# Seven-product up projections: one PSUM bank that sums four products, weights split 1024 wide, and context vectors left out of a modulation

## The chip, the cores and the metric

The kernel runs on one core of a Trainium2 chip. The core's engines work side by side, each through its own queue in order: TensorE (PE) multiplies matrices into PSUM, an accumulator memory of eight banks here; VectorE (DVE) and ScalarE (ACT) do elementwise work between PSUM and SBUF; SyncE (SP) issues the loads. The metric is device microseconds (us) of one execution, as the median of several runs.

## The reference

Two layers over 512 latent tokens and 256 context tokens of width 1024. Each layer has a gated feed-forward block (FFN), a mixer (attention in the first layer, gated linear attention in the second) and another FFN; each adds to the stream through a gate, after a norm with shift and scale that depend on conditioning vectors.

```python
def swiglu(h, w_gu, w_down):
    gu = h @ w_gu
    return (jax.nn.silu(gu[..., :D_FF]) * gu[..., D_FF:]) @ w_down

def pre_mod(t, m, norm_g, i):
    h = rms_norm(t, norm_g[i]) * (1.0 + m[..., 3 * i + 1, :]) + m[..., 3 * i, :]
    return h, m[..., 3 * i + 2, :]

    mod = (jax.nn.silu(c) @ p["w_mod"] + p["b_mod"])          # latent tokens
    mod_c = (jax.nn.silu(c_ctx) @ p["w_mod"] + p["b_mod"])    # context tokens
    h, gt = pre_mod(x, mod, ng, 0)
    x = x + 0.5 * gt * swiglu(h, p["ffn1_w_gu"], p["ffn1_w_down"])
    # ... mixer with ng[1]; FFN 2 with ng[2]; the same for context tokens with mod_c.
    # In the last layer context tokens get no mixer output and no second FFN.
```

`D_FF` is 2816, so a hidden dimension of 22 blocks of 128. Everything is computed in float32 accuracy.

## The kernel before

**Products.** Each float32 operand is split in a high part (rounded, by ScalarE, L127) and a low part (the rest, by VectorE, L128); a product is high x high, high x low and low x high. A weight therefore arrives by DMA in a `raw` tile, and `split` makes `whi` and `wlo` from it. The pool `stage` holds three buffers each of `raw`, `whi` and `wlo`, all [128, 1024], and serves up projections, down projections and projections of the mixers.

**The four FFN stages** (`ffn`) have their units at 117 to 522, 1074 to 1480, 1593 to 1998 and 2408 to 2673 us of the profiled execution. The first three work on all 768 tokens, the last on 512. Within a stage the 22 hidden blocks go in four parts of 6, 6, 5 and 5 (`PARTS`): first the up projections of a part's blocks, then the part's down projections (`pair`, L374), whose results `add_gated` (L398) adds to the stream. The last part's down projections are in `close_out`, which also prepares what follows. From the fifth hidden block on (the sixth in the last stage) the up projection of a block is a `unit`: the weight block A (gate and up columns, two `raw` tiles of 1024) and the activations B are cut in four quarters each, and seven products of quarter sums take the place of eight. The quarter sums of B are made once per stage (T1 to T4); those of A (S1 to S4) in each unit. A product is 4 x 3 matmuls (`product`, L602) of 384 columns, 256 in the last stage: 84 matmuls a unit.

**A unit before** takes four banks (`a` to `d`) of a ring of eight. Two products accumulate in each of `a`, `c` and `d`; one stands in `b`. VectorE makes S1 to S4 in small tiles (L624) and each quarter is split on its own, 512 columns at a time. ScalarE copies the first product of `a` and of `c` to `v` (L641, L643), VectorE adds the others (`add`, L639, and L648), silu is done in `sg` (L651, L654), one VectorE product of 768 columns joins both halves (L658), and `split` makes the hidden block's `dh` and `dl`, which the down projections read.

**The modulation** is worked out piecemeal beside all this: `mod_step` (L278) takes pieces from `pending` at a rate `bg` per unit or down projection, loads 256 KB (`wm`), and has VectorE reduce it against each of two vectors, latent and context (`junk`, L297).

**The order.** The code is written unit by unit, and a scheduler then orders each engine's instructions by its own estimate of times. So matmuls of a next unit may stand between those of the present one. Engines wait for each other where a tile is read, and where its buffer was used before.

Of the kernel before, what the change touches and what calls it, by code (L numbers as in the profile page):

```python
# [8 lines left out]
F32 = mybir.dt.float32  # L9
# [38 lines left out]
class Net:  # L48
# [123 lines left out]
    def mod_finish(self, l, p):  # L172
# [4 lines left out]
        for v in range(2):  # L177
# [4 lines left out]
        if p % 3 == 2 and p != 5:  # L182
            nc.vector.tensor_scalar(out=m, in0=m, scalar1=0.5, scalar2=None, op0=ALU.mult)

# [93 lines left out]
    def mod_step(self, n):  # L278
        nc = self.nc
        self.owed += n  # L280
        while self.owed >= 1 and self.pending:
            self.owed -= 1
            l, p, m, i = self.pending.pop(0)
            if i == 0 and m == 0 and p == 0:
                nc.sync.dma_start(out=self.bmod[l], in_=self.ins[f"b_mod{l}"])
                nc.sync.dma_start(out=self.ng[l], in_=self.ins[f"norm_g{l}"])
# [7 lines left out]
            for v in range(2):  # L294
# [4 lines left out]
            if i and m == KT - 1:  # L299
                nc.vector.tensor_tensor(out=self.mod[l][p], in0=self.mod[l][p], in1=self.acc, op=ALU.add)  # L300
# [151 lines left out]
    def ffn(self, l, sub, idx, segs, nxt, bg=(0, 0), first=4, start=False):  # L452
# [12 lines left out]
        st = ExitStack()  # L465
        with st:
# [52 lines left out]
            for pi, (f0, nf) in enumerate(PARTS):  # L519
                for f in range(f0, f0 + nf):  # L520
                    if f >= early:
                        if f >= first:
# [6 lines left out]
                            seven(sp, gu[f], sg, hid[f])  # L529
# [22 lines left out]
    def seven_open(self, st, h, n0):  # L552
# [7 lines left out]
        sub = lambda o, a, b: nc.vector.tensor_tensor(out=o, in0=a, in1=b, op=ALU.subtract)  # L560

# [26 lines left out]
        def weights(a):  # L588
            hi = self.stage.tile([128, 1024], F32R, tag="whi", name="whi", bufs=3)
            lo = self.stage.tile([128, 1024], F32R, tag="wlo", name="wlo", bufs=3)  # L590
            res = []
            for i, x in enumerate(a):
                c = slice(i * 512, (i + 1) * 512)
                self.split(x(), hi[:, c], lo[:, c])
                res.append((hi[:, c], lo[:, c]))
            return res
# [21 lines left out]
        def unit(sp, src, sg, hid):  # L618
            A11, A12, A21, A22 = [x[:, i:i + 512] for x in [self.raw(src[:, j:j + 1024]) for j in (0, 1024)] for i in (0, 512)]

            def comb(a, b, op):
                def f():
                    o = sp.tile([128, 512], F32, tag="s", name="s", bufs=2)
                    nc.vector.tensor_tensor(out=o, in0=a, in1=b, op=op)  # L624
                    f.out = o
                    return o
                return f
            s1 = comb(A21, A22, ALU.add)
            wA11, wS1 = weights([lambda: A11, s1])
            s2 = comb(s1.out, A11, ALU.subtract)  # L630
# [1200 lines left out]
```

## Time and profile before

| | |
|---|---|
| median of 3 runs | 2709.84 us (2709.37 to 2710.6) |
| profiled execution | 2708.46 us |
| its span, first to last instruction | 2706.7 us |
| mean granted TensorE clock | 0.990 |
| TensorE busy | 2617.1 us (97%) |
| VectorE busy | 2161.1 us (80%) |
| ScalarE busy | 1196.9 us (44%) |
| GpSimd busy | 171.6 us (6%) |
| data moved | 279.31 MB, mean 103 GB/s |

Times of single instructions come from the profiled execution; its time is 1.4 us under the median. Matmuls overlap one another, so their pace is read from one start to the next and not from a duration. "Idle before" in a row is the time for which the engine stood still ahead of that instruction, and the name behind the arrow is what released it. In the mixers TensorE has many small holes; in the FFN stages it has few.

### The profile page before, as it was taken

To read this page: it belongs to the slowest core of one execution; us is meant where nothing else is said; L and a number is where in the kernel's file an instruction comes from. 1 tells how busy PE (TensorE), PEld (TensorE's weight loads), DVE (VectorE), ACT (ScalarE), POOL (GpSimd) and SP (SyncE) were. 2 spreads that over 40 slices of the span, in tenths; PEclk is the share of its full clock that TensorE was granted. 3 is DMA by queue.
4 is the path that set the end of the run, shared out by engine and by line. 5 is a ranking of instruction groups with operands and counts; after the bars stand their busy time and mean duration, and the time that the engine had idled before them with its cause. 6 is when DMAs were issued, how large, how long until landed. Compare 5 with 4: busy or idle time off the path is not lost. (4 is left out here: it accounts for less than half of the span.)

```text
span 2706.7 us, 44030 instructions
## 1 busy us (share of the span) xinstructions
PE 2617.1 (97%) x16800; PEld 2435.1 (90%) x16800; DVE 2161.1 (80%) x4503; ACT 1196.9 (44%) x2254; POOL 171.6 (6%) x206
## 2 busy tenths in 40 slices
PE   7999999999878899999999999999999999999999
PEld 5899999989777789899999999999998998989899
DVE  6789798977888867797988878888777677778677
ACT  4324242445757744242424542424345565435344
POOL 0000000013443200000000000000000121000000
PEclk9999999999989999999999999999999999999999
DMA  8143444431000140433343314343232121422334
GB/s 313 42 150 115 139 132 145 124 126 42 24 24 1 47 141 30 129 114 127 117 141 100 115 63 138 108 145 104 92 116 86 56 71 63 148 71 92 102 106 128
DMA packets 103572, 279.31 MB, mean 103 GB/s; under 512 B 12256, under 2 KB 15200, under 8 KB 101824
## 3 DMA queue, kind: packets, MB, share of 16 engines
q1 hardware_dynamic: 103360, 276.50, 31.4%
q8 instruction: 132, 2.16, 0.3%
q14 instruction: 80, 0.66, 0.1%
HBM read 269.11 MB, written 7.34 MB: 102 GB/s over the span
## 5 line engine op out<-in xcount | busy, mean ns | idle before, releaser
L127 ACT ACTIVATE whi<-raw 128x512 fp32r<-128x512 f32 (+3 forms) x466 | 355.7, 767 | 739.9 <-PE r L374 326.4
L128 DVE TENSOR_TENSOR wlo<-raw,whi 128x512 fp32r<-128x512 f32 (+3 forms) x466 | 399.2, 859 | 81.0 <-ACT whi L127 78.2
L602 PE MATMUL r<-t,whi 128*128 128x384 f32 (+1 forms) x1704 | 400.9, 323 | 1.8 <-DVE u L639 1.3
L602 PE MATMUL r<-hh,wlo 128*128 128x384 f32 (+1 forms) x1136 | 366.1, 323 | 0.0
L602 PE MATMUL r<-hh,whi 128*128 128x384 f32 (+1 forms) x1136 | 365.8, 322 | 0.0
L602 PE MATMUL r<-hl,whi 128*128 128x384 f32 (+1 forms) x1136 | 365.7, 322 | 0.0
L297 DVE SCALAR_TENSOR_TENSOR junk<-wm,cb 128x512 bf16<-128x512 f32 x480 | 329.1, 686 | 13.4 <-ACT cb L276 8.3
L602 PEld LDWEIGHTS r<-t,whi 128*128 128x128 f32 x1704 | 295.6, 188 | 3.2 <-DVE u L639 2.1
L602 PE MATMUL r<-t,wlo 128*128 128x384 f32 (+1 forms) x852 | 273.3, 323 | 0.0
L374 PE MATMUL r<-dh,whi 128*128 128x512 f32 (+1 forms) x952 | 267.3, 345 | 0.8 <-ACT whi L127 0.8
L374 PE MATMUL r<-dh,wlo 128*128 128x512 f32 (+1 forms) x952 | 266.8, 346 | 0.3 <-DVE wlo L128 0.3
L374 PE MATMUL r<-dl,whi 128*128 128x512 f32 (+1 forms) x952 | 266.8, 344 | 0.0
L127 ACT ACTIVATE whi<-s 128x512 fp32r<-128x512 f32 x284 | 174.6, 625 | 182.4 <-DVE s L624 67.0
L602 PEld LDWEIGHTS r<-hl,whi 128*128 128x128 f32 x1136 | 213.4, 188 | 0.8
L602 PEld LDWEIGHTS r<-hh,wlo 128*128 128x128 f32 x1136 | 213.4, 188 | 0.4 <-DVE wlo L128 0.4
L602 PEld LDWEIGHTS r<-hh,whi 128*128 128x128 f32 x1136 | 213.3, 188 | 0.3
L374 PEld LDWEIGHTS r<-dh,wlo 128*128 128x128 f32 x952 | 178.6, 188 | 24.4 <-DVE wlo L128 1.1
L374 PEld LDWEIGHTS r<-dh,whi 128*128 128x128 f32 x952 | 178.0, 188 | 24.5 <-ACT whi L127 2.7
L374 PEld LDWEIGHTS r<-dl,whi 128*128 128x128 f32 x952 | 178.1, 188 | 23.5
L128 DVE TENSOR_TENSOR wlo<-s,whi 128x512 fp32r<-128x512 f32 x284 | 190.7, 684 | 4.4 <-ACT whi L127 3.7
L398 DVE SCALAR_TENSOR_TENSOR x<-r,mod,x 128x512 f32<-128x512 f32 (+1 forms) x168 | 100.1, 632 | 90.8 <-PE r L374 90.3
L602 PEld LDWEIGHTS r<-t,wlo 128*128 128x128 f32 x852 | 159.9, 188 | 0.1
(417 smaller groups left out, 5845.1 us busy)
## 6 DMA issues: line engine op xcount, KB each, us to landing
raw<-gu SPq DMA_DIRECT2D x176, 512.0 KB, 3.9
wm<-w_mod SPq DMA_DIRECT2D x240, 256.0 KB, 2.9
raw<-dn SPq DMA_DIRECT2D x88, 320.0 KB, 2.9
raw<-dn SPq DMA_DIRECT2D x64, 384.0 KB, 3.1
raw<-w_out SPq DMA_DIRECT2D x28, 512.0 KB, 3.8
m<-w_mod0a SPq DMA_DIRECT2D x12, 1024.0 KB, 10.4
raw<-w_in SPq DMA_DIRECT2D x8, 512.0 KB, 4.8
raw<-w_kq SPq DMA_DIRECT2D x8, 512.0 KB, 3.7
```

What stands on the lines that cost most here:

```text
L127: self.nc.scalar.activation(out=hi, in_=src, func=AF.Copy)
L128: (e or self.nc.vector).tensor_tensor(out=lo, in0=src, in1=hi.bitcast(F32), op=ALU.subtract)
L297: nc.vector.scalar_tensor_tensor(out=junk, in0=w, scalar=1.0, in1=self.cb[:, v, :], op0=ALU.mult, op1=ALU.mult, accum_out=self.acc[:, m, v ...
L374: nc.tensor.matmul(out=outs[s][j], lhsT=w[j][wi][:, k * 128:(k + 1) * 128], rhs=xk[k][xi][:, s0:s1], start=(k == 0 and i == 0), stop=(k == ...
L398: self.nc.vector.scalar_tensor_tensor(out=self.xs[m][:, s0:s1], in0=regs[s][j], scalar=gate[:, m, v:v + 1], in1=self.xs[m][:, s0:s1], op0= ...
L602: nc.tensor.matmul(out=o, lhsT=y[wi], rhs=x[k][xi], start=first and k == 0 and i == 0, stop=last and k == H - 1 and i == 2, skip_group_che ...
```

## The change

The unit is rewritten (`mult`, `copy` and `add` are now its small helpers):

- Three banks instead of four. `b` takes the products with A11, S2, S3 and A22, one summed on the other; between them ScalarE copies the sum so far to `v` or `u3`. `c` takes S1 and S4, with a copy between; `a` takes A12 alone. The products' order is A11, A12, S2, S1, S3, S4, A22.
- Four ScalarE copies (were two), three VectorE additions (were five), two VectorE products of 384 columns, one reading `b` (was one of 768).
- Weights are split 1024 wide: A11 with A12, S1 with S2, S3 with A22; S4 alone, 512 wide. S3 and S4 are written in place into the `raw` tiles; S1 and S2 into one tile of 1024.
- The modulation of layer 1 from its sixth vector on is worked out for the latent vector alone (`mod_vectors`), since the reference has no context token there; a piece with one vector counts as half a piece in the rate.

Lines move: products L602 to L609, `pair` L374 to L381, `add_gated` L398 to L405, `junk` L297 to L303. The diff's core:

```diff
+    def mod_vectors(self, l, p):
+        return 1 if l == 1 and p >= 5 else 2
...
-            self.owed -= 1
             l, p, m, i = self.pending.pop(0)
+            nv = self.mod_vectors(l, p)
+            self.owed -= nv / 2
...
-            for v in range(2):
+            for v in range(nv):
                 junk = self.mp.tile([128, D // 2], BF16, tag="junk", name="junk", bufs=1)
...
-            for i, x in enumerate(a):
-                c = slice(i * 512, (i + 1) * 512)
-                self.split(x(), hi[:, c], lo[:, c])
-                res.append((hi[:, c], lo[:, c]))
-            return res
+            n = x.shape[-1]
+            self.split(x, hi, lo)
+            return [(hi[:, c:c + 512], lo[:, c:c + 512]) for c in range(0, n, 512)]
...
-            wA11, wS1 = weights([lambda: A11, s1])
-            wS2, wS3 = weights([s2, s3])
-            wA12, wS4 = weights([lambda: A12, s4])
-            wA22, = weights([lambda: A22])
-            a, b, c, d = [self.bank()[:, 0:n] for _ in range(4)]
+            s = sp.tile([128, 1024], F32, tag="s", name="s", bufs=1)
+            S1, S2 = s[:, 0:512], s[:, 512:1024]
+            wA11, wA12 = weights(raw[0])
+            add(S1, A21, A22)
+            sub(S2, S1, A11)
+            wS1, wS2 = weights(s)
+            sub(A21, A11, A21)
+            wS3, wA22 = weights(raw[1])
+            sub(A12, A12, S2)
+            wS4, = weights(A12)
+            a, b, c = [self.bank()[:, 0:n] for _ in range(3)]
...
-            product(a, wA11, B11, True, True)
-            nc.scalar.activation(out=v[:, 0], in_=a, func=AF.Copy)
-            product(c, wS1, T1, True, True)
-            nc.scalar.activation(out=v[:, 1], in_=c, func=AF.Copy)
-            product(b, wS2, T2, True, True)
-            add(v[:, 0], b, v[:, 0])
-            product(d, wS3, T3, True, True)
-            add(u3, d, v[:, 0])
-            nc.vector.tensor_tensor(out=v[:, 1], in0=u3, in1=v[:, 1], op=ALU.add)
-            product(a, wA12, B21, False, True)
-            nc.scalar.activation(out=g1, in_=a, func=AF.Silu)
-            product(c, wS4, B22, False, True)
-            add(g2, c, v[:, 0])
-            nc.scalar.activation(out=g2, in_=g2, func=AF.Silu)
-            product(d, wA22, T4, False, True)
-            add(v[:, 0], d, v[:, 0])
-            nc.vector.tensor_tensor(out=g, in0=g, in1=v.rearrange("p a n -> p (a n)"), op=ALU.mult)
+            product(b, wA11, B11, True, True)
+            copy(v[:, 0], b)
+            product(a, wA12, B21, True, True)
+            add(g1, a, v[:, 0])
+            nc.scalar.activation(out=g1, in_=g1, func=AF.Silu)
+            product(b, wS2, T2, False, True)
+            copy(v[:, 1], b)
+            product(c, wS1, T1, True, True)
+            copy(v[:, 0], c)
+            product(b, wS3, T3, False, True)
+            copy(u3, b)
+            add(u3, u3, v[:, 0])
+            product(c, wS4, B22, False, True)
+            add(g2, c, v[:, 1])
+            nc.scalar.activation(out=g2, in_=g2, func=AF.Silu)
+            product(b, wA22, T4, False, True)
+            mult(g2, g2, u3)
+            mult(g1, b, g1)
```

Three places show how the scheduler's order moves. A number behind a name tells one tile from another: `t..` and `hh..`, `hl..` are quarters of the activations.

TensorE before, where the first unit of the first stage's second part meets the second (`r_3300` is the first unit's bank `c`, `r_3450` the second unit's `a`; `whi_3420` is in the buffer that `whi_3276` had, 26 matmuls earlier):

```order
L602 MATMUL r_3300<-hh6_130,wlo_3287 128x384
L602 MATMUL r_3300<-hh7_132,whi_3286 128x384
L602 MATMUL r_3300<-hl7_133,whi_3286 128x384
L602 MATMUL r_3300<-hh7_132,wlo_3287 128x384
L602 MATMUL r_3450<-hh0_118,whi_3420 128x384
L602 MATMUL r_3450<-hl0_119,whi_3420 128x384
```

TensorE after at the same seam (`r_3218` and `r_3219` are the first unit's `b` and `c`, `r_3361` and `r_3360` the second unit's `b` and `a`; `whi_3340` is in the buffer of `whi_3203`):

```order
L609 MATMUL r_3218<-t03_754,whi_3203 128x384
L609 MATMUL r_3218<-t13_755,whi_3203 128x384
L609 MATMUL r_3218<-t03_754,wlo_3204 128x384
L609 MATMUL r_3219<-t03_754,wlo_3204 128x384
L609 MATMUL r_3361<-hh0_118,whi_3340 128x384
L609 MATMUL r_3361<-hl0_119,whi_3340 128x384
L609 MATMUL r_3360<-hh4_126,whi_3340 128x384
L609 MATMUL r_3360<-hl4_127,whi_3340 128x384
L609 MATMUL r_3218<-hh0_118,whi_3208 128x384
```

Four matmuls of the second unit, on `whi_3340`, now stand between the S2 and S1 products and the S3 product of the first, and the last matmul on `whi_3203` three places ahead of them.

ScalarE after, at the same place:

```order
L127 ACTIVATE whi_3213<-raw_3192 128x512
L648 ACTIVATE sg_3191<-sg_3191 128x384
L127 ACTIVATE whi_3340<-raw_3335 128x1024
L642 ACTIVATE v_3220<-r_3218 128x384
L642 ACTIVATE v_3220<-r_3219 128x384
L642 ACTIVATE u3_3221<-r_3218 128x384
```

The copy of `b` for S2 (the first to `v_3220` here) stands behind the split of `whi_3340`; before, this stretch held splits of 512 and copies of `a` and `c` alone.

VectorE at the end of the first stage, before (`dl_5078` is the low half of the last hidden block, gain and gcol belong to the attention mixer):

```order
L128 TENSOR_TENSOR wlo_5309<-raw_5306,whi_5308 128x640
L658 TENSOR_TENSOR sg_5079<-sg_5079,v_5118 128x768
L732 TENSOR_SCALAR gain_5444<-gain_5444 128x64
L733 TENSOR_SCALAR gcol_5446<-gcol_5446 128x1
L746 CAST sink_p_5460<-sink_f_5458 96x16
L747 COPY sink_5453<-sink_p_5460 1x16
L749 TENSOR_TENSOR sink_f_5458<-sink_f_5458,sink_p_5460 96x16
L746 CAST sink_p_5460<-sink_f_5458 96x16
L747 COPY sink_5453<-sink_p_5460 1x16
L749 TENSOR_TENSOR sink_f_5458<-sink_f_5458,sink_p_5460 96x16
L128 TENSOR_TENSOR dl_5078<-sg_5079,dh_5077 128x768
```

and after:

```order
L128 TENSOR_TENSOR wlo_5092<-raw_5089,whi_5091 128x640
L660 TENSOR_TENSOR sg_4926<-sg_4926,u3_4956 128x384
L660 TENSOR_TENSOR sg_4926<-r_4953,sg_4926 128x384
L739 CAST identb_5288<-ident_109 128x128
L743 MEMSET sink_5291 96x8
L128 TENSOR_TENSOR wlo_5147<-raw_5144,whi_5146 128x640
L128 TENSOR_TENSOR dl_4925<-sg_4926,dh_4924 128x768
L303 SCALAR_TENSOR_TENSOR junk_5056,macc_4629<-wm_5054,cb_3042 128x512
L736 TENSOR_SCALAR gain_5282<-gain_5282 128x64
L737 TENSOR_SCALAR gcol_5284<-gcol_5284 128x1
```

`dl` (now `dl_4925`) stands ahead of the two scalings, and two products of 384 have the place of the one of 768.

## Rows read from the trace of the kernel before

**Rows 1.** The page's engine list: busy us, share of the span, instructions.

```profile
PE 2617.1 (97%) x16800; PEld 2435.1 (90%) x16800; DVE 2161.1 (80%) x4503; ACT 1196.9 (44%) x2254; POOL 171.6 (6%) x206
```

**Rows 2.** Stretches: length, then busy (count) by engine; PEclk, DMA share, GB/s.

```profile
300.00:350.00 50.00, 50.00 (x289) 45.76 (x288) 42.71 (x102) 12.11 (x20) 0.00 (x0) 1.00 0.50 160
500.00:550.00 50.00, 47.05 (x286) 44.37 (x285) 45.20 (x109) 22.53 (x39) 0.00 (x0) 0.97 0.47 142
...
1450.00:1500.00 50.00, 49.15 (x314) 47.94 (x313) 41.42 (x80) 23.44 (x40) 0.00 (x0) 1.00 0.35 104
```

**Rows 3.** Timeline, a unit's last matmul and its reader on VectorE: start, duration.

```profile
1998.37 0.34 PE L602 MATMUL r<-t,wlo 128*128 128x384 f32 x1
...
1998.74 0.56 DVE L639 TENSOR_TENSOR v<-r,v 128x384 f32<-128x384 f32 x1 [0.66 <-PE r L602]
```

**Rows 4.** Timeline at the first stage's end, TensorE and VectorE.

```profile
525.26 0.28 PE L374 MATMUL b<-dl,whi 128*128 128x256 f32 x1
...
525.38 0.28 PE L374 MATMUL b<-dh,wlo 128*128 128x256 f32 x1
...
526.01 0.51 PE L374 MATMUL b<-dh,whi 128*128 128x256 f32 x2 [0.36 <-ACT dh L127]
526.64 0.15 DVE L733 TENSOR_SCALAR gcol<-gcol 128x1 f32<-128x1 f32 x1 [0.86 <-DMA gcol<-gain_col]
...
527.77 0.95 DVE L128 TENSOR_TENSOR dl<-sg,dh 128x768 fp32r<-128x768 f32 x1
...
528.78 0.38 PE L374 MATMUL b<-dl,whi 128*128 128x256 f32 x1 [2.26 <-DVE dl L128]
```

**Rows 5.** What TensorE's instructions waited for: us in total, times, longest.

```profile
PE b L374 <- DVE dl L128: 3.5, 4, 2.3
...
PE r L602 <- DVE u L639: 1.3, 3, 0.8
...
PE r L374 <- ACT whi L127: 0.8, 1, 0.8
```

**Rows 6.** Groups of one line and shape: count; busy us, mean ns; idle before.

```profile
L297 DVE SCALAR_TENSOR_TENSOR junk<-wm,cb 128x512 bf16<-128x512 f32 x480 | 329.1, 686 | 13.4 <-ACT cb L276 8.3
...
L128 DVE TENSOR_TENSOR wlo<-s,whi 128x512 fp32r<-128x512 f32 x284 | 190.7, 684 | 4.4 <-ACT whi L127 3.7
...
L128 DVE TENSOR_TENSOR wlo<-raw,whi 128x1024 fp32r<-128x1024 f32 x93 | 114.2, 1234 | 31.6 <-ACT whi L127 30.8
...
L127 ACT ACTIVATE whi<-raw 128x1024 fp32r<-128x1024 f32 x93 | 97.8, 1057 | 89.5 <-PE a L374 25.9 <-DMA raw<-gu 17.3 <-PE b L374 11.9
...
L639 DVE TENSOR_TENSOR v<-r,v 128x384 f32<-128x384 f32 x108 | 59.7, 552 | 18.2 <-PE r L602 18.0
...
L658 DVE TENSOR_TENSOR sg<-sg,v 128x768 f32<-128x768 f32 x54 | 51.4, 951 | 0.6
...
L641 ACT ACTIVATE v<-r 128x384 f32<-128x384 f32 x54 | 25.7, 475 | 10.4 <-PE r L602 10.4
```

**Rows 7.** Timeline at the second stage's end, ScalarE and TensorE.

```profile
1482.90 0.84 ACT L127 ACTIVATE dh<-sg 128x768 fp32r<-128x768 f32 x1 [1.82 <-DVE sg L658]
...
1483.16 0.28 PE L374 MATMUL b<-dh,wlo 128*128 128x256 f32 x1
1483.80 0.51 PE L374 MATMUL b<-dh,whi 128*128 128x256 f32 x2 [0.36 <-ACT dh L127]
1484.79 0.39 PE L374 MATMUL b<-dl,whi 128*128 128x256 f32 x1 [0.49 <-DVE dl L128]
```

**Rows 8.** Timeline in a part's first unit: a weight buffer changes hands.

```profile
341.95 0.34 PE L602 MATMUL r<-hl,whi 128*128 128x384 f32 x1
...
342.38 0.64 ACT L127 ACTIVATE whi<-raw 128x512 fp32r<-128x512 f32 x1 [3.14 <-issue]
...
346.46 0.34 PE L602 MATMUL r<-hh,whi 128*128 128x384 f32 x1
```

**Rows 9.** The page's DMA issues: count, KB each, us to landing.

```profile
raw<-gu SPq DMA_DIRECT2D x176, 512.0 KB, 3.9
```

More of the change, by code (lines that the diff above doesn't have):

```diff
@@ L176, in mod_finish @@
         bias = self.bmod[l][:, p * KT:(p + 1) * KT]
-        for v in range(2):
+        for v in range(self.mod_vectors(l, p)):
             nc.vector.tensor_tensor(out=m[:, :, v], in0=m[:, :, v], in1=bias, op=ALU.add)
@@ L299, in mod_step @@
             if i and m == KT - 1:
-                nc.vector.tensor_tensor(out=self.mod[l][p], in0=self.mod[l][p], in1=self.acc, op=ALU.add)
+                a, b = [x[:, :, 0:nv] for x in (self.mod[l][p], self.acc)]
+                nc.vector.tensor_tensor(out=a, in0=a, in1=b, op=ALU.add)
                 self.mod_finish(l, p)
@@ L465, in ffn @@
         st = ExitStack()
+        n0 = segs[0][0]
         with st:
@@ L528, in ffn @@
                             sg = pool.tile([128, T], F32, tag="sg", name="sg", bufs=1)
-                            seven(sp, gu[f], sg, hid[f])
+                            seven(sp, gu[f], sg, lambda: self.split(sg[:, n0:T], *[x[:, n0:T] for x in hid[f]]))
                         else:
@@ L560, in seven_open @@
         sub = lambda o, a, b: nc.vector.tensor_tensor(out=o, in0=a, in1=b, op=ALU.subtract)
+        add = lambda o, a, b: nc.vector.tensor_tensor(out=o, in0=a, in1=b, op=ALU.add)
         s2 = ExitStack()
@@ L616, in start, with unit @@
             return self.pool("seven", st)
[L618 to L628, printed above, removed]
-            wA11, wS1 = weights([lambda: A11, s1])
-            s2 = comb(s1.out, A11, ALU.subtract)
-            s3 = comb(A11, A21, ALU.subtract)
-            wS2, wS3 = weights([s2, s3])
-            s4 = comb(A12, s2.out, ALU.subtract)
-            wA12, wS4 = weights([lambda: A12, s4])
-            wA22, = weights([lambda: A22])
-            a, b, c, d = [self.bank()[:, 0:n] for _ in range(4)]
+        def unit(sp, src, sg, done):
+            raw = [self.raw(src[:, j:j + 1024]) for j in (0, 1024)]
+            A11, A12, A21, A22 = [x[:, i:i + 512] for x in raw for i in (0, 512)]
+            s = sp.tile([128, 1024], F32, tag="s", name="s", bufs=1)
[9 more added lines that the diff above has]
+            a, b, c = [self.bank()[:, 0:n] for _ in range(3)]
@@ L645, in unit @@
-            add(v[:, 0], b, v[:, 0])
-            product(d, wS3, T3, True, True)
-            add(u3, d, v[:, 0])
-            nc.vector.tensor_tensor(out=v[:, 1], in0=u3, in1=v[:, 1], op=ALU.add)
-            product(a, wA12, B21, False, True)
-            g1, g2 = sg[:, lo], sg[:, hi]
-            nc.scalar.activation(out=g1, in_=a, func=AF.Silu)
+            copy = lambda o, x: nc.scalar.activation(out=o, in_=x, func=AF.Copy)
+            g1, g2 = sg[:, lo], sg[:, hi]
+            product(b, wA11, B11, True, True)
@@ L654, in unit @@
             nc.scalar.activation(out=g2, in_=g2, func=AF.Silu)
-            product(d, wA22, T4, False, True)
-            add(v[:, 0], d, v[:, 0])
-            g = sg[:, n0:T]
-            nc.vector.tensor_tensor(out=g, in0=g, in1=v.rearrange("p a n -> p (a n)"), op=ALU.mult)
-            self.split(g, hid[0][:, n0:T], hid[1][:, n0:T])
+            product(b, wA22, T4, False, True)
+            mult = lambda o, x, y: nc.vector.tensor_tensor(out=o, in0=x, in1=y, op=ALU.mult)
+            mult(g2, g2, u3)
@@ L661, in seven_open @@
+            mult(g1, b, g1)
+            done()
         return start, unit
```

10 lines of the change are left out of this document (4 added, 6 removed).

## The prediction

> **What bounds the kernel now.** I read the page's engine list first [rows 1]: TensorE is busy 97% of the span. An average over stages doesn't say what a change in one stage is worth, so next come the busy times by stretch [rows 2]. Inside a gated feed-forward (FFN) stage, from 300 to 350, TensorE is busy 50.00 us of 50, while VectorE works 42.71 and ScalarE 12.11 of the same 50. So in the stages that the change touches nothing but the matmul stream sets the time. Its pace: 289 matmuls start in those 50 us, nearly all of 384 columns, 0.173 us each; of 256 columns two start at 525.26 and 525.38 [rows 4], 0.12 us. A unit of seven products is 7 x 12 matmuls: 84 x 0.173 = 14.5 us in the three FFN stages with 384 columns (18 units each), 84 x 0.12 = 10.1 us in the last (17 units with 256 columns).
>
> There are almost no holes. The largest place in these stages is at 526 us [rows 4], and the table of what TensorE waited for [rows 5] holds, for the lines of the units (L602) and of the down projections (L374), sums of a few microseconds in 2,700. Two things follow. VectorE or ScalarE work saved in a unit is worth nothing by itself. And any new dependency that goes out from TensorE and comes back to it must be covered by matmuls placed between, or it lengthens the kernel by what is not covered.
>
> **What the change removes.** Durations by shape are in [rows 6]. In a unit VectorE had seven weight splits of 0.684, five additions of 0.552 and one product of 0.951; now it has three splits of 1.234 and one of 0.684, three additions and two products of 384 columns, which I take as additions. That is 3 x (1.234 - 2 x 0.684) - 2 x 0.552 + (2 x 0.552 - 0.951) = -1.35 us a unit. ScalarE gets two copies more, 2 x 0.475 = 0.95 us, and gives something back with splits of double width. A unit lasts 14.5 us, and both engines have room in it [rows 2]: worth nothing, and no cost either. The context vectors left out take 64 products from VectorE, 64 x 0.686 = 44 us, in the third FFN stage; TensorE is full beside them, so this is nothing too. In that stage the pieces now come at twice the rate, so their 256 KB loads move earlier on the SP queue; DMA stands at a share of 0.35 from 1450 to 1500 [rows 2], which leaves room. The matmuls are equal in number and width, and in the two mixers the order of all engines is nearly the same.
>
> Holes that do go, by the new order:
> - 526 us. There `dl` (the low half of the last hidden block) stands on VectorE behind two scalings, gain and gcol, which wait for their DMA, the second for 0.86 us [rows 4]; TensorE's next matmul starts at 528.78. From 525.38 that is 3.40 us for three steps, 3.40 - 3 x 0.12 = 3.0 us lost. Behind it the granted clock falls: 0.97 as a mean of 50 us [rows 2], 0.03 x 50 = 1.5 us. In the new order `dl` stands ahead of both scalings: -4.5 us. What is late next there is a down weight's low part, below.
> - Two stage ends (1483, 2002). A 768-wide product (0.95) stands between the last sum and `dh`, `dl` [rows 7]: 1483.16 to 1484.79 is 1.63 us for three steps, 1.27 lost; twice -2.5 us. At the kernel's end the same product leaves a chain with no cover: -0.95.
> - Three waits for `u` (1.3 us together) and one of a down projection for `whi` (0.8) [rows 5] have no successor in the new order: -2.1.
> Sum: -10.1 us.
>
> **What it adds: turnarounds.** Bank `b` takes four products, with a copy by ScalarE read out between them, and a 1024-wide split needs a whole weight buffer at once. Both make TensorE wait for something that its own matmul of a moment ago released. The price has three terms: last matmul's start to the reader's start, 1998.37 to 1998.74 = 0.37 us (here VectorE reads it) [rows 3]; the ScalarE instruction, 1.057 for a 1024-wide split, 0.475 for a copy [rows 6]; and the way back, `dh` ends at 1482.90 + 0.84 = 1483.74 and its matmul starts at 1483.80 [rows 7], so 0.06. Less the matmuls that stand between.
>
> Before, there were many between. At 341.95 [rows 8] the last matmul that uses a `whi` buffer starts, at 342.38 (0.43 later) ScalarE's split into that buffer starts, and the first matmul on it is only at 346.46: 26 matmuls between, some 3 us of slack. In the new order the first matmuls of a part's second unit are put between products of its first: their `whi` goes into the buffer that the matmul three places ahead released. That is 0.37 + 1.06 + 0.06 - 3 x 0.173 = 0.97 us of idle TensorE, with nothing else to run. I count, over the whole of the order: ten such places with three matmuls between, 9.7; two with two between, 2 x 1.14 = 2.3; three in the last stage, two matmuls of 0.12 between, 3 x 1.25 = 3.7; two where the copy of `b` stands on ScalarE behind another split, 0.37 + 1.06 + 0.475 + 0.06 - 4 x 0.173 = 1.3 where that split is 1024 wide, a little less where it is 640 wide, so 2.4. The others: the first unit of the third stage, where combinations, `dl` and a 1.234 split follow each other on VectorE, some 6.5 us with 28 matmuls (4.8 us) beside it, 1.7; three waits for a copy of 0.3 to 0.6, 1.3; the two stage ends, where a down projection's bank waits for the last product's reader (0.37 + 0.55 + 0.06 - 0.173), 1.6; and after 526 the low part of a down weight, between 0 and 1.4, which I take at 1.0. Sum: +23.7 us.
>
> Where 0.475 of a copy plus 0.43 (0.9 us) meets a gap in `b`, five or more matmuls between cover it, and that is the usual gap; so most of the 71 units cost nothing, and the cost sits at the seams between one unit and the next.
>
> Net +23.7 - 10.1 = +13.6. The profiled execution took 2708.46 us, so 2722.1 by its own measure; the median of the runs is 1.4 higher, 2723.4. I say **2723**. A price between 0.6 (the reader starting as the matmul ends, without its 0.37) and 1.3 for the seventeen at the seams moves this by some 6 us to either side: 2717 to 2729.
>
> The Trainium skill, "PSUM — Partial Sum Buffer", section "Summary: rules for kernel authors", wants a reader and a running matmul on different banks. Bank `b` breaks that; the sum above already holds its consequence, since the order then forces TensorE to stop. Were each of the three copies out of `b` in all 71 units to stop TensorE for its 0.9 us, that would be 192 us, some 2900; I give it no chance, since the order has matmuls of other banks behind most of them, and such matmuls are cover, as in [rows 8].
>
> **The rivals.**
> *No turnaround binds.* The order is what is issued, but a release could reach ScalarE sooner than I think, or buffers could be handed out so that the seams have slack as in [rows 8]. Then only the holes that go count: 2709.84 - 10.1 = 2699.7, faster. Against it: TensorE has no reserve in these stages (50.00 of 50), and its instructions are issued in order. 0.07.
> *Half of them bind.* 11.9 - 10.1 = +1.8, some 2711.6, no difference by the bound of 0.2% (5.4 us, about what a measurement of this kernel can tell from no change). This is also where the change goes if the seams cost half of what I take. 0.13.
> *The clock falls at the seams.* After the hole at 526 the clock fell and 1.5 us went. If each of some sixteen new holes did that, 16 x 1.5 = 24 us come on top: 2747. Against it: the holes at 1483 [rows 7] were 1.27 us together, longer than one of mine, and the granted clock of 1450 to 1500 stands at 1.00 [rows 2]. 0.06. The Trainium skill, "TensorE: Matmul & The Clock Gate", section "A second HAM failure mode: psum-queue depth-cycling", tells of a matmul kernel whose short pauses between groups on cycling banks made the clock swing; in this trace only the longest pause did.
> *Weights come late in the last stage.* `raw` is now written in place and held until S4 is split, so that its next load starts later; a load lands after 3.9 us [rows 9] and a unit lasts only 10.1 us. If that loop gets longer than the unit by 1 us, 17 units cost 17 us more: 2740. Against it: there are three `raw` buffers for two loads a unit. 0.04.
>
> **How the numbers follow.** Forecast 0.70, the rivals 0.07, 0.13, 0.06 and 0.04. The range reaches from the case of half, 2709, over the forecast's 2717 to 2729, to 2735, which takes in a part of the two dear cases; what it leaves out is the first rival and most of those two, under 0.2. Faster: the first rival and a little of the half case, 0.09. Same: most of the half case and the forecast's low tail, 0.14. Slower: 0.77.
>
> **What would show it.** Right: in the changed profile, waits of the products' line for `whi` at the split, some thirteen with about 0.8 us idle each, all where one part's first unit meets its second; four copies per unit on ScalarE; VectorE's busy time down by about 44 + 71 x 1.3 = 136 us without effect; no hole at 526 and a clock of 0.99 to 1.00 there. Wrong: full TensorE at those seams (first or second rival); a granted clock well below 1 in stretches without a mixer (third); waits for `raw` after 2500 (fourth). The forecast is also wrong if a hole that I count as gone comes back at another instruction of the same chain.

## The result

The changed kernel takes 2745.26 us (median of 4 runs, 2743.16 to 2749.08) against 2709.70 (2709.37 to 2710.60): a ratio of 1.0134, 95% interval 1.0122 to 1.0146, 35.6 us slower. The forecast had the direction, and somewhat over a third of the size: 2723, with 2735 as the range's upper end. The profiled execution of the changed kernel took 2747.05 us, its span 2745.2, so its differences from before (38.5 us of span) are some 3 us larger than those of the medians.

Where the time went is read first from the starts of the units' first and last matmul in each stage (the products' line, L602 before and L609 after), in us:

| | before | after | difference |
|---|---|---|---|
| units of the first stage | 405.1 | 418.1 | +13.0 |
| attention mixer and what lies around it | 551.5 | 549.4 | -2.1 |
| units of the second stage | 406.6 | 412.9 | +6.3 |
| units of the third stage | 404.9 | 418.8 | +13.9 |
| linear attention and what lies around it | 409.5 | 412.4 | +2.9 |
| units of the last stage | 264.7 | 269.1 | +4.4 |

What the table leaves out (the start, the 113 us between the second and the third stage, and the end) differs by 0.1 us together. So the loss is in the units, 37.6 us, and the mixers hardly count. The page's engine list of the changed kernel, beside [rows 1]:

```profile
PE 2629.1 (96%) x16800; PEld 2437.4 (89%) x16800; DVE 2053.6 (75%) x4086; ACT 1235.0 (45%) x2183; POOL 170.9 (6%) x206
```

VectorE works 107 us less than before, without effect, and TensorE is what waits. What TensorE's instructions waited for (us in total, times, longest), the rows that answer to [rows 5]:

```profile
PE r L609 <- ACT whi L127: 20.2, 17, 5.7
...
PE r L609 <- ACT v L642: 4.1, 5, 2.1
...
PE b L381 <- DVE sg L660: 2.8, 4, 0.8
...
PE r L609 <- DVE wlo L128: 2.1, 2, 1.5
...
PE r L609 <- ACT u L642: 1.2, 2, 0.6
```

Before, the units' line had a single kind of wait worth naming, 1.3 us in three. Now ScalarE stands in nearly all of them: 17 times for the high part of a weight, five times for a copy to `v`, twice for a copy to `u` (the tile `u3`). The stretches that answer to [rows 2], and the one from 1700 (length, then busy by engine, granted clock, DMA share):

```profile
300.00:350.00 50.00, 49.15 (x280) 43.88 (x279) 39.12 (x90) 10.86 (x14) 0.00 (x0) 1.00 0.49 152
...
500.00:550.00 50.00, 48.00 (x306) 46.87 (x305) 45.70 (x111) 22.80 (x37) 0.00 (x0) 1.00 0.41 126
1450.00:1500.00 50.00, 47.75 (x277) 46.65 (x276) 41.19 (x79) 24.34 (x37) 0.00 (x0) 1.00 0.28 86
...
1700.00:1750.00 50.00, 44.27 (x248) 43.96 (x248) 39.95 (x75) 23.00 (x34) 0.00 (x0) 0.97 0.52 163
```

From 300 to 350, where TensorE had no hole, one of 0.85 us now stands; from 1700 to 1750 nearly 6 us are missing, and the clock with them. At 500 to 550 the clock is back at 1.00, as forecast. Three kinds of holes follow, each with its rows.

**A seam.** TensorE and ScalarE where a part goes from its first unit to its second, the place of [rows 8]. By the starts of the units it is the first stage's third part (units from 338 to 421 us), not the second, as the text on the change has it:

```profile
345.89 0.51 PE L609 MATMUL r<-t,whi 128*128 128x384 f32 x2
346.24 0.51 PE L609 MATMUL r<-t,wlo 128*128 128x384 f32 x2
347.59 0.44 PE L609 MATMUL r<-hh,whi 128*128 128x384 f32 x1 [0.85 <-ACT whi L127]
```

```profile
346.48 1.06 ACT L127 ACTIVATE whi<-raw 128x1024 fp32r<-128x1024 f32 x1 [0.46 <-DMA raw<-gu]
347.45 0.85 ACT L642 ACTIVATE v<-r 128x384 f32<-128x384 f32 x2
```

The matmul that releases the buffer is the second of the pair at 345.89, so it starts near 346.06 (one pace later). ScalarE's split starts 0.42 later, lasts 1.06, and TensorE goes on at 347.59. Here the profile puts the split's wait down to a DMA; the distance is that of [rows 8], 0.43, and at another seam of the same run the profile names TensorE:

```profile
497.16 1.06 ACT L127 ACTIVATE whi<-raw 128x1024 fp32r<-128x1024 f32 x1 [3.58 <-PE r L609]
```

After the hole the next matmul starts 0.28 later and not 0.17. From start to start (346.41, the second of the pair at 346.24, to 347.59) the seam costs 1.01 us over the pace, and 1.01 + 0.11 = 1.12 us with the second matmul.

**The hole at 1707.** SyncE, ScalarE and TensorE at the first seam of the third stage, again between a part's first unit and its second:

```profile
1699.76 0.80 SPq L280 DMA_DIRECT2D cb<-c_row  x2
...
1704.87 1.06 ACT L281 ACTIVATE cb<-cb 128x1024 f32<-128x1024 f32 x1 [2.98 <-DMA cb<-c_row]
1705.83 1.04 ACT L127 ACTIVATE whi<-raw 128x1024 fp32r<-128x1024 f32 x1
```

```profile
1706.92 0.69 PE L609 MATMUL r<-hh,whi 128*128 128x384 f32 x1 [5.73 <-ACT whi L127]
1707.41 0.52 PE L609 MATMUL r<-hl,whi 128*128 128x384 f32 x1
1707.73 0.52 PE L609 MATMUL r<-hh,whi 128*128 128x384 f32 x1
1708.05 0.52 PE L609 MATMUL r<-hl,whi 128*128 128x384 f32 x1
```

`cb` is the conditioning row, of which the modulation needs the second half from here on. Its silu starts 5.1 us after the load's issue, as soon as the load has landed, and the split that TensorE needs stands behind it in ScalarE's queue. Afterwards the matmuls start 0.32 us apart: the clock is at its lower level, 1.2 GHz, for a while. From 1700.86, the last start ahead of it, the place costs 7.4 us over the pace.

**A copy behind silu.** The first stage at 380, VectorE, ScalarE and TensorE:

```profile
376.35 0.85 ACT L127 ACTIVATE dh<-sg 128x768 fp32r<-128x768 f32 x1 [1.85 <-DVE sg L660]
...
377.23 0.96 DVE L128 TENSOR_TENSOR dl<-sg,dh 128x768 fp32r<-128x768 f32 x1 [0.31 <-ACT dh L127]
...
378.10 0.69 DVE L303 SCALAR_TENSOR_TENSOR junk<-wm,cb 128x512 bf16<-128x512 f32 x1
...
378.71 0.55 DVE L569 TENSOR_TENSOR sg<-r,v 128x384 f32<-128x384 f32 x1
...
379.36 0.52 ACT L648 ACTIVATE sg<-sg 128x384 f32<-128x384 f32 x1 [2.17 <-DVE sg L569]
...
379.79 0.47 ACT L642 ACTIVATE v<-r 128x384 f32<-128x384 f32 x1
```

```profile
380.32 0.44 PE L609 MATMUL r<-hh,whi 128*128 128x384 f32 x1 [2.15 <-ACT v L642]
```

The copy takes 0.47 us. It starts late because silu stands ahead of it, silu waits for VectorE's sum, and that waits in VectorE's queue behind the previous unit's `dl` and a piece of the modulation. Together 2.4 us.

### The profile page after: what moved, and what is told of

Its sections match the earlier page's. It is cut to its first block, busy times and chain, and to the rows that moved or that the text cites. A ratio compares the mean times of both kernels' runs of the same rounds, so it can differ in the third digit from the quotient of the medians.

```text
span 2745.2 us, 43465 instructions
## 1 busy us (share of the span) xinstructions
PE 2629.1 (96%) x16800; PEld 2437.4 (89%) x16800; DVE 2053.6 (75%) x4086; ACT 1235.0 (45%) x2183; POOL 170.9 (6%) x206
## 5 line engine op out<-in xcount | busy, mean ns | idle before, releaser
L127 ACT ACTIVATE whi<-raw 128x1024 fp32r<-128x1024 f32 (+3 forms) x466 | 416.3, 897 | 709.6 <-PE r L381 310.5
L128 DVE TENSOR_TENSOR wlo<-raw,whi 128x1024 fp32r<-128x1024 f32 (+3 forms) x466 | 476.9, 1026 | 129.4 <-ACT whi L127 125.7
L609 PE MATMUL r<-t,whi 128*128 128x384 f32 (+1 forms) x1704 | 401.0, 323 | 1.3 <-ACT u L642 1.2
L609 PE MATMUL r<-hh,whi 128*128 128x384 f32 (+1 forms) x1136 | 369.0, 326 | 24.9 <-ACT whi L127 20.2
L609 PE MATMUL r<-hl,whi 128*128 128x384 f32 (+1 forms) x1136 | 365.9, 323 | 0.0
L609 PE MATMUL r<-hh,wlo 128*128 128x384 f32 (+1 forms) x1136 | 354.0, 323 | 0.8 <-DVE wlo L128 0.6
L303 DVE SCALAR_TENSOR_TENSOR junk<-wm,cb 128x512 bf16<-128x512 f32 x416 | 285.9, 687 | 28.2 <-ACT cb L281 12.8
L609 PEld LDWEIGHTS r<-t,whi 128*128 128x128 f32 x1704 | 295.2, 188 | 3.2 <-ACT u L642 1.8
L609 PE MATMUL r<-t,wlo 128*128 128x384 f32 (+1 forms) x852 | 270.3, 323 | 1.5 <-DVE wlo L128 1.5
L381 PE MATMUL r<-dh,wlo 128*128 128x512 f32 (+1 forms) x952 | 271.3, 348 | 0.0
L381 PE MATMUL r<-dl,whi 128*128 128x512 f32 (+1 forms) x952 | 268.4, 345 | 0.0
L381 PE MATMUL r<-dh,whi 128*128 128x512 f32 (+1 forms) x952 | 267.4, 345 | 0.0
L609 PEld LDWEIGHTS r<-hh,whi 128*128 128x128 f32 x1136 | 213.9, 188 | 33.0 <-ACT whi L127 25.3
L609 PEld LDWEIGHTS r<-hl,whi 128*128 128x128 f32 x1136 | 214.0, 188 | 1.3
L609 PEld LDWEIGHTS r<-hh,wlo 128*128 128x128 f32 x1136 | 211.7, 188 | 1.9 <-DVE wlo L128 1.9
L381 PEld LDWEIGHTS r<-dh,whi 128*128 128x128 f32 x952 | 178.2, 188 | 25.8 <-ACT whi L127 2.0
L381 PEld LDWEIGHTS r<-dh,wlo 128*128 128x128 f32 x952 | 178.5, 188 | 22.6
L381 PEld LDWEIGHTS r<-dl,whi 128*128 128x128 f32 x952 | 178.2, 188 | 22.6
L405 DVE SCALAR_TENSOR_TENSOR x<-r,mod,x 128x512 f32<-128x512 f32 (+1 forms) x168 | 100.2, 632 | 104.6 <-PE r L381 104.2
L609 PEld LDWEIGHTS r<-t,wlo 128*128 128x128 f32 x852 | 158.9, 188 | 1.9 <-DVE wlo L128 1.8
L127 ACT ACTIVATE whi<-s 128x1024 fp32r<-128x1024 f32 x71 | 75.4, 1062 | 144.7 <-PE r L609 57.3
L642 ACT ACTIVATE v<-r 128x384 f32<-128x384 f32 (+1 forms) x213 | 96.1, 457 | 83.1 <-PE r L609 76.6
```

What stands on the lines that cost most here:

```text
L127: self.nc.scalar.activation(out=hi, in_=src, func=AF.Copy)
L128: (e or self.nc.vector).tensor_tensor(out=lo, in0=src, in1=hi.bitcast(F32), op=ALU.subtract)
L303: nc.vector.scalar_tensor_tensor(out=junk, in0=w, scalar=1.0, in1=self.cb[:, v, :], op0=ALU.mult, op1=ALU.mult, accum_out=self.acc[:, m, v ...
L381: nc.tensor.matmul(out=outs[s][j], lhsT=w[j][wi][:, k * 128:(k + 1) * 128], rhs=xk[k][xi][:, s0:s1], start=(k == 0 and i == 0), stop=(k == ...
L405: self.nc.vector.scalar_tensor_tensor(out=self.xs[m][:, s0:s1], in0=regs[s][j], scalar=gate[:, m, v:v + 1], in1=self.xs[m][:, s0:s1], op0= ...
L609: nc.tensor.matmul(out=o, lhsT=y[wi], rhs=x[k][xi], start=first and k == 0 and i == 0, stop=last and k == H - 1 and i == 2, skip_group_che ...
```

## The experiments

The theory that the runs test: three costs, all through ScalarE's queue, (1) some seventeen seams of 1.1 to 1.3 us, (2) the moved silu of the conditioning row, 6 us more than a seam, (3) copies of bank `b` behind instructions that wait. Rivals: bank `b` costs by its own turnaround in every unit; the wide splits cost by themselves; the vectors left out matter. Of each set of runs the kernel before ran on the same chip; its median is given.

### The vectors alone, on the kernel before

The part of the diff on `mod_vectors` and `owed`, put into the kernel before; units, banks and splits stay.

> The kernel before with one part of the change alone: the context vector left out of the layer-1 modulation from the sixth vector on, at the halved piece price that the change has. ScalarE's silu of the second half of the conditioning row (cb) moves forward in its queue, to just ahead of the weight split that a part's second unit needs. Theory A (the vectors are worth nothing by themselves, and the moved silu hurts only as far as matmuls don't cover it; in the four-bank unit 26 matmuls, 4.5 us, stand between the release of that buffer and its use, against a wait of 4 to 5 us for the row's DMA plus 1.06 us): 2710 to 2713, with one hole of 0 to 3 us near 1700. Rival B (44 us of VectorE work saved are worth something): below 2707. Rival C (the moved silu costs its whole 6 us here too): 2716.

The run took 2716.56 against 2710.99 us: ratio 1.0023 (1.0014 to 1.0032), 5.6 us slower. SyncE, ScalarE and TensorE there:

```profile
1680.15 0.80 SPq L280 DMA_DIRECT2D cb<-c_row  x2
...
1687.07 1.06 ACT L281 ACTIVATE cb<-cb 128x1024 f32<-128x1024 f32 x1 [10.53 <-DMA cb<-c_row]
1688.04 0.61 ACT L127 ACTIVATE whi<-raw 128x512 fp32r<-128x512 f32 x1
...
1688.70 0.69 PE L609 MATMUL r<-hh,whi 128*128 128x384 f32 x1 [4.77 <-ACT whi L127]
```

```profile
1650.00:1700.00 50.00, 45.23 (x245) 42.09 (x244) 39.16 (x90) 12.64 (x22) 0.00 (x0) 0.93 0.60 186
```

Rival C was right: the whole price, in a unit with four banks and 26 matmuls of cover. The row's load was issued at 1680.15 and its silu began at 1687.07; no cover of 4.5 us lasts that long. So this part of the change loses 5 to 6 us by itself. By these rows it loses them because it moves one ScalarE instruction, which takes 1.06 us, to a place where the next weight stands behind it.

### The changed kernel with the old rate

```diff
-            self.owed -= nv / 2
+            self.owed -= 1
```

> The changed kernel, with a piece of the modulation counted as a whole piece again, so that the rate is that of before and the silu of the second half of cb goes back to where it stood on ScalarE; the context vectors stay left out. Theory A (the 5.7 us hole at 1707 is the split queued behind that silu, which waits for the row's DMA): that hole shrinks to the 0.85 us of its neighbours, and the half clock behind it goes: 2738 to 2740, 6 us less than the changed kernel. Rival B (that hole belongs to the seam or to the weights' DMA): 2745, with a hole over 4 us still there.

2738.01 against 2710.99: ratio 1.0104 (1.0087 to 1.0121), 27.0 us over before where the changed kernel has 35.6. The third stage's units take 412.9 us in place of 418.8; the seam at 1700 costs 1.12 us like its neighbours. What TensorE waited for:

```profile
PE r L609 <- ACT whi L127: 15.7, 17, 1.1
...
PE r L609 <- ACT v L642: 3.7, 3, 2.5
```

This is theory A: 17 waits as before, the longest now 1.1 in place of 5.7. Of the 8.6 us by the medians the profile shows 5.9; the rest lies within the spread of the runs (6 us from run to run in the changed kernel).

### The vectors alone with the old rate, on the kernel before

The same line in the kernel of the first experiment.

> The kernel before with the context vectors left out, a piece counted whole, so that the silu of the conditioning row stays where it was. Theory A (64 products less on VectorE are worth nothing under a full TensorE; what the run with one vector lost was the moved silu): the same as before, within 2 us. Rival B (leaving out the vectors costs by the moved loads and order as such): 4 us or more above before.

2710.97 against 2709.67: ratio 1.0005 (0.9996 to 1.0014). Leaving 64 products out of VectorE is worth nothing, as forecast, and what cost in the first experiment came with the faster rate; its rows put it at the moved silu.

### Units in order

On the kernel with the old rate; of a unit's matmuls only the first may still pass the ones written ahead of it.

```diff
-                    nc.tensor.matmul(out=o, lhsT=y[wi], rhs=x[k][xi], start=first and k == 0 and i == 0,
+                    mm = nc.tensor.matmul(out=o, lhsT=y[wi], rhs=x[k][xi], start=first and k == 0 and i == 0,
                                      stop=last and k == H - 1 and i == 2, skip_group_check=not first)
+                    if w is not self.w0 or k or i:
+                        self.tc.keep_in_program_order(mm)
...
             wA11, wA12 = weights(raw[0])
+            self.w0 = wA11
```

> As the run with the old rate, and the matmuls of a unit from its second product on (all but the first product's first matmul) are pinned on TensorE behind those written ahead of them, so that no matmul of a next unit stands between the S2 and S3 products. Theory A (the seams cost because next-unit matmuls are drawn into the gap of bank b, onto a weight buffer released three matmuls earlier; with 12 matmuls of another bank between, each copy of 0.9 us is covered): no waits for whi of 0.85 or 1.0 us at the units' line, holes of the FFN stages together about 9 us against some 12 of before: 2703 to 2710, about 30 us under the changed kernel. Rival B (each copy out of bank b or each 1024-wide split costs by itself, wherever the matmuls stand): 2730 or more.

2721.89 against 2710.99: ratio 1.0042 (1.0028 to 1.0056). That is 16 us less than with the old rate alone, and the waits are now

```profile
PE r L609 <- ACT v L645: 7.2, 6, 3.7
...
PE r L609 <- ACT whi L127: 1.7, 3, 0.8
```

The 17 waits for `whi` are three. Ten seams of 1.12, three of 1.29 and three of 1.34 us, as the run with the old rate has them, make 19: the seams come from matmuls of the next unit that were drawn between the products of this one, and go when these are kept out. Bank `b`, the copies and the wide splits are all still there, so rival B falls as the main cause. But the kernel is 11 us slower than before, where theory A had it at 2703 to 2710: the copies' waits went up. The longest, at the third stage's first unit:

```profile
1598.22 1.06 ACT L281 ACTIVATE cb<-cb 128x1024 f32<-128x1024 f32 x1 [1.53 <-DMA cb<-c_row]
1599.19 1.04 ACT L127 ACTIVATE whi<-raw 128x1024 fp32r<-128x1024 f32 x1
1600.13 0.47 ACT L645 ACTIVATE v<-r 128x384 f32<-128x384 f32 x1
...
1600.66 0.62 PE L609 MATMUL r<-t,whi 128*128 128x384 f32 x2 [3.69 <-ACT v L645]
```

Again silu of the row, and behind it a split and the copy of `b` that TensorE needs.

### The copies ahead of what waits

On the kernel with the units in order.

```diff
-            nc.scalar.activation(out=g1, in_=g1, func=AF.Silu)
             product(b, wS2, T2, False, True)
             copy(v[:, 1], b)
+            self.tc.keep_in_program_order(nc.scalar.activation(out=g1, in_=g1, func=AF.Silu))
...
     def mod_half(self, i):
-        nc.scalar.activation(out=self.cb, in_=self.cb, func=AF.Silu)
+        self.cb_raw = True
```

`cb_silu`, called at the next `mod_step`, does the row's silu, pinned in ScalarE's order.

> As the run with the units in order, and on ScalarE two instructions that wait are taken out of the copies' way: silu of the first half (which waits for VectorE's sum) is pinned behind the copy of b after S2, and the silu of the conditioning row (which waits for its DMA) is issued one piece step after its load. Theory A (what is left over in the run in order are copies queued behind these two: 1.4, 1.2 and 5.5 us at the stages' first units, 1.0, 0.8 and 1.0 us behind silu): 11 us less than that run, 2709 to 2713, about the kernel before. Rival B (what is left is the turnaround of bank b itself, in all units): 2718 or more.

2714.18 against 2709.67: ratio 1.0017 (1.0008 to 1.0026), 4.5 us over before where the run in order has 10.9. TensorE's waits:

```profile
PE r L621 <- ACT v L657: 1.7, 2, 1.1
...
PE r L621 <- DVE wlo L128: 0.6, 2, 0.4
```

That is theory A in kind, just over its range, with 6.4 of the 11 us; how much of it each of the two edits gave was not tried apart. The first two stages' units take 405.9 and 406.4 us, like before (405.1, 406.6). The third still has 407.8 against 404.9, half of the difference in one hole at its start, and the last 268.1 against 264.7, in many holes of 0.3 us. So bank `b` needs no more time than four banks in units of 14.5 us, if nothing that waits stands ahead of its copies; in units of 10 us a rest of 3.4 us stays, whose cause was not tried apart.

### Narrow splits with bank b

On the kernel with the old rate: `weights` and the combinations as in the kernel before, the products and copies as after.

> As the changed kernel with the old rate, but with the weights of before: seven splits of 512, paired as before, combinations in small tiles; bank b and its ScalarE copies stay. Theory A (bank b is what costs, and how much depends on what ScalarE has in its queue ahead of a copy: by the order some sixty waits of 0.2 to 4 us, together 56 us against 25 for the wide splits, since more and later instructions stand ahead of the copies): 2765 to 2780, with most waits on the copy (v) and few on whi. Rival B (the wide splits are what costs at the seams): 2715 to 2722.

2769.95 against 2709.67: ratio 1.0223 (1.0209 to 1.0237), 60 us slower.

```profile
PE r L611 <- ACT v L648: 31.5, 30, 3.8
...
PE r L611 <- ACT whi L127: 6.0, 14, 0.6
```

This is theory A: without the wide splits bank `b` loses more than twice as much, so the wide splits are not what makes bank `b` dear. TensorE waits thirty times for a copy, about 1 us each. In 23 of the thirty a silu that waits for VectorE's sum stands ahead of the copy in ScalarE's queue, as here:

```profile
226.06 0.52 ACT L654 ACTIVATE sg<-sg 128x384 f32<-128x384 f32 x1 [3.47 <-DVE sg L569]
...
226.50 0.47 ACT L648 ACTIVATE v<-r 128x384 f32<-128x384 f32 x1
...
227.02 0.44 PE L611 MATMUL r<-hh,whi 128*128 128x384 f32 x1 [1.16 <-ACT v L648]
```

In the other seven ScalarE stood free, the copy started as soon as its product released it, and TensorE waited 0.58 us for the turnaround of the bank itself.

### Two narrow instructions in place of each wide one

```diff
-            self.split(x, hi, lo)
+            for c in range(0, n, 512):
+                self.split(x[:, c:c + 512], hi[:, c:c + 512], lo[:, c:c + 512])
```

> As the changed kernel with the old rate; each 1024-wide split is written as two instructions of 512 into the same buffers (high and low part each). Theory A (where the scheduler then puts matmuls and copies decides: by the order some forty waits of together 37 us against 25, because four narrow splits or a silu now stand ahead of a copy): 2745 to 2755. Rival B (at a seam only the duration of the split counts, 1.06 us, of which the first half alone would be 0.63): 0.43 us less at each of some fifteen seams, 2731.

2752.15 against 2709.60: ratio 1.0158 (1.0145 to 1.0172), 14 us more than with the wide ones (15.5 by the difference from before).

```profile
PE r L610 <- ACT whi L127: 13.1, 23, 0.9
PE r L610 <- ACT v L643: 10.3, 8, 3.1
```

The kernel's time is theory A's, but at the seams rival B is right to the hundredth: nine of the ten seams of 0.85 us now wait 0.42.

```profile
210.95 0.45 PE L610 MATMUL r<-hh,whi 128*128 128x384 f32 x1 [0.42 <-ACT whi L127]
```

So a seam does last as long as the split that it waits for. The gain is lost elsewhere. The last stage has ten waits of 0.66 us in place of three of 1.08, and with other small ones its units take 278.3 us in place of 268.1; and two copies stand behind a silu that waits, 3.12 us at 128 and 2.26 at 1098, so that the copies' wait nearly triples. The order that the scheduler makes of the new instructions costs more than the shorter split gives.

### Wide splits with four banks

On the kernel with the old rate: the products, additions and copies of before, with the weights of after.

> As the run with the old rate, but with the four banks, the additions and the copies of the unit before; the weights stay split 1024 wide and in place. Theory A (the seams need the copies of bank b: with four banks the matmuls of a next unit come later, but a 1024-wide split still comes later than two of 512, which opens some twenty waits of 0.1 to 1.6 us for VectorE's sums and low parts, 21 us by the order where the kernel before has 11): 2718 to 2724. Rival B (the wide splits alone make the seams): 2738. Rival C (bank b is the only cause): 2709 to 2711.

2733.21 against 2710.99: ratio 1.0085 (1.0070 to 1.0099), 22 us slower. That is none of the three: the sixteen waits at seams are gone (four waits for `whi`, 4.7 us together), so rival B falls, but the kernel is 9 us above theory A. Its profile has 18 us more than before in the units, in many waits of 0.2 to 0.7 us and one place of 6 us at the third stage's start, and 8 in and around the mixers, where the wait for `dl` at the first stage's end grew from 2.3 to 3.3 us. Each part of the change by itself loses, 5.6, 22 and 60 us, and no sum of the parts gives the whole: what one part puts into a queue decides what the other waits for.

### Two attempts at a better kernel

On the kernel before with one vector at the old rate. First the operations on gain, gcol and sink from VectorE to GpSimd, and two products of 384 columns in place of the one of 768.

> As the run with one vector and the old rate, on the kernel before with its four banks and narrow splits, with two edits at the stages' ends: the small operations of the attention mixer that wait for DMAs (gain, gcol, sink) go to GpSimd, so that dl doesn't queue behind them, and the 768-wide product becomes two of 384, the first ahead of the last sum. Theory A (the hole at 526 and the half clock behind it go, the stage ends shrink by 0.4 each): 4 to 6 us under before. Rival B (another wait, of a down weight's low part, takes the hole's place): within 2 us of before.

2709.55 against 2709.67: the same (0.9992 to 1.0009). The hole did go, as TensorE's waits for `dl` show beside 3.5 us in [rows 5]:

```profile
PE b L381 <- DVE dl L128: 1.7, 4, 0.5
```

But the last stage's units took 267.4 us (264.7 before) and the linear attention 412.0 (409.5). So the time is rival B's, and the place is neither theory's. Then the same with the last stage's product as before:

> As the run with gain, gcol and sink on GpSimd, but the two products of 384 only in the three stages with 384 columns; the last stage keeps its product of 512. Theory A (the last stage's 2.7 us that the run with GpSimd gave back came from the order of that product's parts): 2.5 us less than that run, 3 us under before. Rival B (those 2.7 us came with the GpSimd operations or are chance): the same as before within 1 us.

2707.88 against 2709.60, ratio 0.9994 (0.9985 to 1.0003): faster by 1.7 us at the most likely, and not told from none. The last stage's units are back at 265.1 us, as theory A had it. No kernel here clearly beats the one before.

## Why the prediction was wrong in size

**Direction and seams: right.** The forecast had seventeen places of this kind, 18.1 us. The profile has sixteen waits for `whi` at seams, of 1.12, 1.29 or 1.34 us from start to start (the one at 1707 is among them), and one copy behind a split 640 wide (528.74, 1.35 us), together 20.4 us at the seams' normal price. The 17 in the table of waits is another count: its seventeenth, at 1331, is no seam. The three terms held: 0.42 us to the reader, 1.06, and back. What the working left out is that the second matmul after a hole starts 0.11 us later than the pace: a seam costs 1.12 in place of 0.97. Three seams have two matmuls between, where the forecast had two such seams. Keeping the units in order took 16 us off.

**The step that failed: "so this is nothing too".** The context vectors left out were costed by what they take from VectorE and by their loads. I followed the moved loads along the SP queue and not the instruction that waits for them on ScalarE. With the faster rate the silu of the second half of the row came to stand ahead of a seam's split, 7.4 us in place of the 1 us that I had there. The kernel before with this part alone loses 5.6 us; with the old rate, nothing. This step alone doesn't explain the miss: with the old rate the changed kernel is still 27.0 us over before, and the range ended 25 us over it.

**The step that was mis-sized: "three waits for a copy of 0.3 to 0.6, 1.3".** In the first stage these three came to 0.83, 2.42 and 0.47, 3.7 us. The chain was the right one, silu behind a VectorE sum behind `dl`, and its length was underestimated. That the usual gap in `b` covers its copies, so that "most of the 71 units cost nothing", held, but cover was counted from the matmul to the copy, as if ScalarE stood free. Holes came up that I had not listed: at 1495 and 2027 for copies to `u` (0.85 us each), at 1331 for a split (0.92), at 1626 for a low part (0.89). With the first stage's end (0.92, which I had not listed) and many small ones in the last stage (some 2.5) that is some 7 us that the sum had not.

**What was to go: partly.** The hole at 526 went with its clock, and 0.92 us at the stage's own end came in its place; the low part of a down weight cost a wait of 0.25 us at 544, not 1.0. The stage ends fell from 1.27 to 0.92 each. The 0.95 us at the kernel's end did not come: the last stage's product has 512 columns and takes 0.68 us, not 0.95, and the stretch behind the last unit's last matmul grew, from 34.1 to 34.8 us. The linear attention lost 2.9 us, for which I had nothing; it took between 409.3 and 412.3 us in the other runs, so how much of this belongs to the change stays open. VectorE's busy time fell by 107 us, not 136.

Together: 13.6 forecast, about +2.3 for the seams, +6.3 for 1707, +2.4 for the three copies, +7 for the unlisted, +1.6 at the kernel's end and +2.9 at the linear attention make 36. The profiled executions, from which these rows come, differ by 38.5 us, so some 2 us have no row here.

**The rivals.** No turnaround binds, and half of them bind: refuted by sixteen waits for `whi` at seams and a copy's wait. Ten of the sixteen lie where a part's first unit meets its second, as forecast; six (266.61, 498.26, 1460.97 and the last stage's three) lie between later units. The clock at the seams: refuted, 1.00 in the stretches at 300, 500 and 1450, which hold one to three such holes each; in the units it fell once, behind 5.7 us. The Trainium skill, "TensorE: Matmul & The Clock Gate", section "A second HAM failure mode: psum-queue depth-cycling", has short pauses between groups as a cause of such swings; these rows don't show it for pauses of 0.85 to 1.08 us. That only the longest pause made the clock swing, as the prediction has it, holds for the FFN stages alone; in the attention mixer of the kernel before, with many waits of at most 2.2 us, the clock fell too:

```profile
700.00:750.00 50.00, 41.28 (x259) 34.64 (x258) 42.07 (x109) 36.10 (x92) 25.69 (x34) 0.88 0.06 22
```

The prediction's remark that bank `b` breaks the rule that it cites on banks is not borne out either: at the seam shown above the copy of `b` at 347.45 runs beside matmuls on other banks, and the next product on `b` starts at 348.40, after it. Weights late in the last stage: its units lost 4.4 us, of which three seams are 4.0, and not 17. The range's upper end came from the last two rivals, and what went over it was neither of them, but the part that I had costed at nothing and the copies and holes that the sum had too small or not at all.

## What to carry to other kernels

A copy out of PSUM on an in-order engine costs what stands ahead of it: before moving such a copy, list what that engine will have queued there and which of it waits for a DMA, a buffer or another engine. Where a change alters a rate or a due time, follow every instruction that hangs on it, the small one that waits for the load above all, to its new neighbours. And where a scheduler sets the order, the parts of a change can't be added up: here they lost 5.6, 22 and 60 us alone, and together 36. Nor does a shorter instruction at the place that waits help by itself, if the order around it changes.

## What the runs showed of the hardware

- After a hole the second matmul starts 0.28 us after the first, and not 0.17, at every seam with 384 columns (347.59 and 347.87): 0.11 us a hole; with 256 columns it is 0.22 and not 0.12. It is so also where TensorE waited for a copy (380.32 and 380.60). The weight load (PEld) of the first matmul starts only with it, at 380.31, while in the stream a load starts 0.17 us ahead of its matmul, as at 380.60 below. That this is the reason no run tests.

```profile
380.31 0.19 PEld L609 LDWEIGHTS r<-hh,whi 128*128 128x128 f32 x1 [2.47 <-ACT v L642]
...
380.60 0.19 PEld L609 LDWEIGHTS r<-hh,wlo 128*128 128x128 f32 x1
380.77 0.34 PE L609 MATMUL r<-hh,wlo 128*128 128x384 f32 x1
```

- Holes and the clock, in the FFN stages: waits of 5.73 us (changed kernel), 4.77 (one vector), 3.82 and 3.65 (narrow splits), 3.69 (units in order) and 3.12 (two narrow instructions) each left the lower clock level behind them, and so did [rows 4], where a wait of 2.26 stands 2 us behind others. Single waits of 2.15 us (changed kernel, 380), 2.47 (old rate, 378), 2.30 (narrow splits, 128), 2.23 and 2.26 (two narrow instructions, 384 and 1098) and all seams of 0.85 to 1.08 did not.
- The conditioning row's broadcast load of two pieces, issued at 1680.15 in one run and 1699.76 in another, was ready for silu 6.9 and 5.1 us later, while weights were loading beside it at 160 to 190 GB/s.
